# The down projection of a decoder layer, product by product over all pairs of k tiles, with operands formed earlier and read back from DRAM

## The chip, the core and the metric

The kernel runs on one core of one Trainium2 chip. The time is what the device takes for one execution, in microseconds (us), and the figure that counts is the median of several executions. The core's engines are told by their names in the profile: PE (matrix products; PEld its weight loads), DVE (vector), ACT (scalar), POOL (GpSimd), SP (which here only issues transfers). SBUF is the memory on the core, PSUM the eight banks that PE writes, DRAM the memory outside.

## The reference

One inference step of one hybrid decoder layer for 1024 prompt tokens and 32 sample tokens (1056 columns in all), all in float32. The part that matters here is the end of the layer, the gated MLP and the final norm:

```
up = rmsnorm(x, ln2) @ ffn_up                    # 1024 -> 2 * 2816
upc, ff_new = causal_dwconv(up, ff_prev, ffn_conv_w)
gate, val = jnp.split(upc, 2, axis=-1)
x = x + (jax.nn.silu(gate) * val) @ ffn_down     # 2816 -> 1024
y = rmsnorm(x, ln_f)
```

What comes before (three parallel mixers: attention, a short convolution, a gated delta net; their gates and the output projection) is computed by the same kernel and is left as it is.

## The kernel before

Everything is kept feature-major: 128 features on the partitions, 1056 tokens along a row. A float32 product is made of three products of float32r parts: every operand is split into hi and lo (`split`, L216: ACT casts hi, then DVE or POOL subtracts to get lo), and PE forms hi\*hi + hi\*lo + lo\*hi. One such matmul is 128x128 by 264 columns (a quarter of the tokens, HU; half of them, 528 columns, is HT).

Background work is written as generators, "lanes", that a loop advances by one step at each `bg.tick()` between matmuls, or without matmuls in `bg.until(cond)`. SBUF slots come from two arenas, `col` (24 slots) and `bg` (18). A lane that wants slots waits until there are enough. So the order in which the lanes were written out, and how many slots are free, fix the order of instructions on each engine; the engines take theirs strictly in that order. All loads and stores of the last stages go through SP's queue, except the weights, which ACT's queue issues.

The stages at the end:

- The up projection (from about 1228 us): 22 steps f, each with seven products in Winograd's form of Strassen's recursion (halves of features, of k tiles, and of tokens). While step f+1 runs, the lane `halves(f)` does the convolution, the SiLU and the product of step f, and writes the hidden features of k tile f to `hid_d[f]`.
- The down projection (`down_phase`, L2329) in the same form: pairs p of k tiles (2p, 2p+1), seven products i of sums of their quarters. Ten of eleven pairs are done so, in groups of 3, 4 and 3. Within a group, product i of all its pairs is summed in eight PSUM banks, and at the end of each group and product the eight banks are added to sums in SBUF (L2366 to L2368). The operands are made as the work goes on: `down_produce` (L2257) forms on DVE the sum of weights (L2286) and the sum of hidden features (L2291) that a product needs, then splits both (weights' lo on POOL, hidden features' lo on DVE). `together` (L2311, L2317) adds the partial sums to the residual `x1`.
- The last two k tiles (`last_group`, L2423, matmuls at L2437) without the recursion, by token groups, and behind each group the final norm of its token blocks (`final_block`, transposes at L2409).

Of the kernel before, what the change touches and what calls it, by code (L numbers as in the profile page):

```python
# [6 lines left out]
F32 = mybir.dt.float32  # L7
# [34 lines left out]
def shape_constants():  # L42
    """Identity, triangles and masks: they depend on the shapes alone."""
# [31 lines left out]
class Lanes:  # L75
    """Background work, traced in steps between the matrix products of the projections."""
# [45 lines left out]
class Arena:  # L122
    """SBUF slots of one size; a slot is free again after its tile's last use."""
# [27 lines left out]
XT_ACT = 1, 4, 7   # k tiles whose x^T the scalar engine copies  # L151
# [9 lines left out]
v b3 k q1 q2 q3 attn_in attn z0 z1 z2 z3  # L161
# [5 lines left out]
DITEM, DAHEAD = 4, 3  # L167
KEEP = 1
# [5 lines left out]
def trunk(tc, A, O, cst_d):  # L174
# [40 lines left out]
    def split(src, hi, lo, eng):  # L215
        """hi + lo == src exactly, each in the 12 significant bits that float32r carries."""  # L216
# [12 lines left out]
    # matrices of q = head * 8 + chunk: A's diagonal and off-diagonal blocks, (I + A)^-1 of the diagonal ones, U  # L229
# [23 lines left out]
    smallT = cp.tile([128, 40], F32, name="smallT")  # L253
# [48 lines left out]
    def look():  # L302
        """The next weights, from within a step."""
# [16 lines left out]
    def products(ps, wh, wl, xh, xl, nk, tg):  # L320
        """ps[:, :TG] = w.T @ x over nk k tiles: float32 products of exact hi + lo parts."""
# [18 lines left out]
    def group(tg):  # L340
        """columns of the group, its prompt columns, its samples"""
# [4 lines left out]
    def padded(t, K):  # L346
        """[128, 8, K - 1 + 4] view of the samples' rows behind the padded prompt."""
# [3 lines left out]
    def conv(src, K, w, out):  # L351
        """Causal depthwise conv along the padded columns; out column o reads o .. o + K - 1."""
# [8 lines left out]
    def conv_samples(t, K):  # L361
        """[128, 8, 4] view of the samples' columns of a conv output."""
# [3 lines left out]
    def state_in(src, rows, nct, dst, name):  # L366
        """(rows, nct * 128) -> dst[128, nct * rows], columns (ct, row), through the tensor engine."""
# [19 lines left out]
    def state_out(src, R, nct, pr, out_p, out_s, name):  # L387
        """src[128, nct * R], per ct pr prompt rows, then the samples' rows, to the two state outputs."""
# [24 lines left out]
    # =============== h = rmsnorm(x), feature-major, as hi + lo ===============  # L413
# [10 lines left out]
    ss, rs, fs = smallT[:, 4:13], smallT[:, 13:22], smallT[:, 22:40]  # L424
# [1715 lines left out]
    def halves(f, gc, uc):  # L2140
# [44 lines left out]
        if f >= NFT - 2:  # L2185
            ta.drop()
# [301 lines left out]
```

## Time and profile before

| what | value |
|---|---|
| median of 3 runs | 1954.34 us (1954.75, 1948.69, 1954.34) |
| span of the profiled execution | 1948.5 us |
| that span against the runs | 0.2 us below the lowest of them, 5.8 us below the median |
| PE busy in the span | 1820.2 us (93%) |
| DVE busy | 1360.4 us (70%) |
| POOL busy | 1017.4 us (52%) |
| ACT busy | 793.9 us (41%) |
| DRAM and SBUF traffic | 251.24 MB, 129 GB/s on average |

A row that begins with an interval gives the busy time of each engine in it and, in brackets, its number of instructions; PEclk is the mean granted clock of PE as a share of full speed. In a row of a group of instructions come the busy time, the mean duration of one in ns, and the idle time of the engine just before them with what ended it. An overlap of pipelined matmuls makes the duration of one longer than the distance between two.

### The profile page before, as it was taken

How to read it: one execution, taken by the hardware profiler on the slowest of the kernel's cores; microseconds unless marked ns; L12 is line 12 of the kernel's file. 1: busy time of each engine (PE TensorE's matmuls, PEld its weight loads, DVE VectorE, ACT ScalarE, POOL GpSimd, SP SyncE). 2: the span in 40 equal slices, each digit the busy share in tenths (PEclk: the TensorE clock that was granted, in tenths of full speed). 3: DMA queues.
4: the chain of work that ended last, by engine and by line, in shares of the span. 5: the costliest groups of instructions: out<-in, count | busy, mean ns of one | idle time of the engine just before them, and what ended most of it. 6: DMA issues, size and time to landing. Idle time of an engine off the chain costs nothing. (4 is left out here: it accounts for less than half of the span.)

```text
span 1948.5 us, 33487 instructions
## 1 busy us (share of the span) xinstructions
PE 1820.2 (93%) x12822; PEld 1760.5 (90%) x12822; DVE 1360.4 (70%) x2385; ACT 793.9 (41%) x1644; POOL 1017.4 (52%) x936
## 2 busy tenths in 40 slices
PE   6999899989999999989898999999999999989878
PEld 5888799989989998989787998999999999879877
DVE  5689845822447677766999757766666667986895
ACT  5654511011124444334544455545545444523312
POOL 1565666613213213363568547777777774544761
PEclk8999999988999999989999999999999999999979
DMA  6312876475745436432553342222322226512102
GB/s 218 108 60 84 286 230 192 107 192 163 228 126 152 135 101 202 166 109 96 202 179 111 121 144 88 87 79 67 99 67 83 82 67 238 190 36 100 45 12 106
DMA packets 265471, 251.24 MB, mean 129 GB/s; under 512 B 55698, under 2 KB 225150, under 8 KB 265294
## 3 DMA queue, kind: packets, MB, share of 16 engines
q1 hardware_dynamic: 209278, 208.20, 33.2%
q10 hardware_dynamic: 56032, 40.90, 7.0%
q8 instruction: 101, 1.65, 0.3%
q14 instruction: 60, 0.49, 0.1%
HBM read 176.23 MB, written 74.82 MB: 129 GB/s over the span
## 5 line engine op out<-in xcount | busy, mean ns | idle before, releaser
L326 PE MATMUL mm<-col,wh 128*128 128x352 f32 x2424 | 607.0, 329 | 17.5 <-DVE col L1203 13.7
L326 PEld LDWEIGHTS mm<-col,wh 128*128 128x128 f32 x2424 | 428.3, 191 | 26.1 <-issue 11.3
L326 PE MATMUL mm<-col,wl 128*128 128x352 f32 x1224 | 401.5, 328 | 0.0
L218 POOL TENSOR_TENSOR wl<-wr,wh 128x1024 fp32r<-128x1024 f32 x50 | 124.0, 2479 | 238.6 <-ACT wh L217 209.4
L326 PEld LDWEIGHTS mm<-col,wl 128*128 128x128 f32 x1224 | 232.9, 190 | 2.8 <-issue 0.5
L217 ACT CAST wh<-wr 128x1024 fp32r<-128x1024 f32 (+2 forms) x100 | 79.7, 803 | 178.4 <-PE mm L326 157.2
L218 POOL TENSOR_TENSOR wl<-col,wl 128x512 fp32r<-128x512 f32 (+1 forms) x78 | 101.8, 1305 | 96.2 <-ACT wl L217 89.3
L218 POOL TENSOR_TENSOR wh<-col,wh 128x512 fp32r<-128x512 f32 (+1 forms) x74 | 97.4, 1316 | 73.1 <-ACT wh L217 63.9
L1449 DVE TENSOR_TENSOR bgps<-bgps,col 128x264 f32<-128x264 f32 x136 | 59.2, 437 | 96.9 <-PE bgps L1421 91.7
L1421 PE MATMUL mm<-bg,wh 128*128 128x264 f32 x744 | 114.0, 289 | 7.4 <-DVE wh L218 2.5
L1421 PE MATMUL mm<-col,wh 128*128 128x264 f32 x648 | 105.1, 290 | 10.9 <-ACT col L1430 5.2
L1421 PE MATMUL mm<-bg,wl 128*128 128x264 f32 x720 | 109.3, 288 | 4.6 <-DVE wl L218 2.2
L1421 PEld LDWEIGHTS mm<-bg,wh 128*128 128x128 f32 x744 | 100.8, 192 | 9.5 <-DVE wh L218 2.9
L1421 PEld LDWEIGHTS mm<-bg,wl 128*128 128x128 f32 x720 | 96.9, 191 | 5.9 <-DVE wl L218 2.4
L1421 PEld LDWEIGHTS mm<-col,wh 128*128 128x128 f32 x648 | 90.4, 193 | 12.8 <-ACT col L1430 5.8
L1421 PE MATMUL mm<-col,wl 128*128 128x264 f32 x576 | 95.1, 292 | 6.8 <-POOL wl L218 3.3
L217 ACT CAST wh<-col 128x512 fp32r<-128x512 f32 (+1 forms) x86 | 48.1, 562 | 113.7 <-PE bgps L1421 59.0
L1421 PEld LDWEIGHTS mm<-col,wl 128*128 128x128 f32 x576 | 81.4, 194 | 8.0 <-POOL wl L218 3.5
L359 DVE SCALAR_TENSOR_TENSOR col<-col,vecT 128x1080 f32<-128x1080 f32 (+1 forms) x44 | 81.7, 1873 | 5.1 <-ACT col L357 3.3
L1421 PE MATMUL bgps<-col,wl 128*128 128x264 f32 x528 | 84.2, 288 | 1.0 <-POOL wl L218 1.0
L1203 DVE TENSOR_TENSOR col<-mm,bg 128x352 f32<-128x352 f32 x84 | 43.4, 517 | 56.6 <-PE mm L326 56.4
L217 ACT CAST wl<-col 128x512 fp32r<-128x512 f32 (+1 forms) x92 | 51.9, 566 | 75.1 <-PE mm L2355 32.2
(578 smaller groups left out, 4964.0 us busy)
## 6 DMA issues: line engine op xcount, KB each, us to landing
wr<-in_w_in SPq DMA_DIRECT2D x44, 512.0 KB
g_d<-col SPq DMA_DIRECT2D x24, 528.0 KB
wr<-in_ffn_up ACTq DMA_DIRECT2D x22, 512.0 KB
col<-in_ffn_up ACTq DMA_DIRECT2D x22, 512.0 KB
hid_d<-col SPq DMA_DIRECT2D x21, 512.0 KB
bg<-qkv_d SPq DMA_DIRECT2D x40, 256.0 KB
col<-g_d SPq DMA_DIRECT2D x18, 528.0 KB
col<-hid_d SPq DMA_DIRECT2D x13, 528.0 KB
```

The source lines that it names most:

```text
L217: nc.scalar.copy(hi, src)
L218: eng.tensor_tensor(lo, src, f32(hi), op=ALU.subtract)
L326: mm(ps[:, :TG], a[:, k, :], b[k][:, cc], start=n == 0, stop=n == last)
L359: nc.vector.scalar_tensor_tensor(out[:, :L], src[:, j:j + L], w(j), out[:, :L], op0=ALU.mult, op1=ALU.add)
L1203: nc.vector.tensor_tensor(dst[:, cc], ps[:, :TG], rr1[:, cc], op=ALU.mult)
L1421: mm(ps, w[:, x + k, :], b[y][:, c0:c0 + HU], start=not n and piece not in NESTED, stop=n == last, skip_group_check=piece in NESTED)
L1449: nc.vector.tensor_tensor(dst, ps, x, op=ALU.add)
```

## The change

The down projection is written anew. All eleven pairs take part in the recursion. One product is done for all eleven pairs before the next begins (order t1, b22, b11, t2, t3, t4, b21), summed over the pairs in eight PSUM banks. A chain of products goes on in the same banks: t1 then b22, and b11 then t2, t3, t4; where a product ends, the banks are added to the right quarter of the residual, while the sum in them goes on. So `together`, the sums in SBUF over groups and the last group without recursion are gone. The last product, b21, is done by token quarters, and the final norm follows behind.

The operands of a product and a pair are one item, and they are read from DRAM as they are needed: a quarter of weights (128x512) and of hidden features (128x528), or sums of such quarters. The sums of weights are formed by a new lane `weight_sums` on POOL, beside the attention and the gates; the sums of hidden features by `halves` on DVE, behind each odd step f of the up projection. `down_load` reads eight items ahead, `down_produce` splits four ahead. All of these transfers are on SP's queue. The `bg` arena has 21 slots instead of 18; the scratch memory for DMA descriptors is set to 1024.

```diff
-N_COL, N_BG = 24, 18
+N_COL, N_BG = 24, 21
-DITEM, DAHEAD = 4, 3
+DITEM, DAHEAD, DLOAD = 4, 4, 8
...
-v b3 k q1 q2 q3 attn_in attn z0 z1 z2 z3
+v b3 k q1 q2 q3 attn_in attn sums z0 z1 z2 z3
...
+    def weight_sums():
+        for p in range(NPAIR):
+            yield sb.room(3)
+            wa, wb, s = (sb.take([128, 1024]) for _ in range(3))
+            for i, w in enumerate((wa, wb)):
+                dma(w, A["ffn_down"][0][(2 * p + i) * 128:(2 * p + i + 1) * 128, :])
+            yield bg.arrived()
...
+            tt = nc.gpsimd.tensor_tensor
+            tt(s1, a21, a22, op=ALU.add)
+            tt(s2, s1, a11, op=ALU.subtract)
+            yield
+            tt(a21, a11, a21, op=ALU.subtract)
+            tt(a12, a12, s2, op=ALU.subtract)
+            yield bg.after(4.0)
+            for x, t in (("t1", s1), ("t2", s2), ("t3", a21), ("b22", a12)):
+                dma(sw_d[x][p], t)
...
     def halves(f, gc, uc):
...
-        dma(hid_d[f][:, 0:SEQ], gv[:, 0:SEQ])
-        dma(hid_d[f][:, SEQ:T], h.rearrange("p b t -> p (b t)"))
+        nc.scalar.copy(bt(gv[:, SEQ:T]), h)
...
+        if f % 2 == 0:
+            dma(hp_d["b11"][p], gv[:, :HT])
+            first_hid[p] = gv, va
+            return
...
+        for x, c in (("b21", 0), ("b22", HT)):
+            dma(hp_d[x][p], gb[:, c:c + HT])
...
+        sub(t1, b12, b11)
+        dma(hp_d["t1"][p], t1)
+        yield between
+        sub(t2, b22, t1)
+        dma(hp_d["t2"][p], t2)
+        yield between
+        sub(b12, b22, b12)
+        dma(hp_d["t3"][p], b12)
+        yield between
+        sub(b11, b21, t2)
+        dma(hp_d["t4"][p], b11)
...
-    GROUPS = (3, 4, 3)
...
+    def down_load(j):
+        while dn["loaded"] <= min(j, len(items) - 1):
+            n = dn["loaded"]
+            x, p = items[n]
+            bg.until(lambda: room2(1)() and (n >= NPAIR or done.get("hid", 0) > p))
+            t, ta = grab([128, SLOT])
+            w, b = t[:, 0:512], t[:, 512:512 + HT]
...
+            dma(w, src)
+            dma(b, hp_d[x][p])
...
+    def down_produce(j):
...
+            b, ba = grab([128, T], F32R)
+            split(bs, b[:, :HT], b[:, HT:T], nc.vector)
+            split(ws, w[:, :512], w[:, 512:], nc.gpsimd)
...
-    def together():
...
+    def down_mm(ps, w, b, mp, u, start, stop):
...
+        mm(ps, hi, bh, start=start, stop=False, skip_group_check=True)
+        mm(ps, hi, bl, start=False, stop=False, skip_group_check=True)
+        mm(ps, lo, bh, start=False, stop=stop, skip_group_check=True)
+
+    def down_out(x, ps, mp, u):
+        dm, c = DOUT[x]
+        o = x1[mp + dm][:, c + u * HU:c + (u + 1) * HU]
+        with tc.high_priority(offset=PRI_PAIR):
+            nc.vector.tensor_tensor(o, o, ps, op=ALU.add)
...
     def down_phase():
...
+        for j in range(end):
+            x, p = items[j]
+            down_load(j + DLOAD)
+            down_produce(j + DAHEAD)
...
+            for n, (mp, u) in enumerate(tiles):
...
+                down_mm(ps, w, b, mp, u, p == 0 and x in ("t1", "b11"), p + 1 == NPAIR)
+                if p + 1 == NPAIR:
+                    down_out(x, ps, mp, u)
+                bg.tick(us=0.33)
...
+        for u in range(2):
...
+            for i in range(3):
+                bg.add(final_block(5 + 3 * u + i, u * HU + 88 * i, 88))
...
-    def last_group():
...
-    nc = _bacc.Bacc("TRN2", target_bir_lowering=False, num_devices=1)
+    nc = _bacc.Bacc("TRN2", target_bir_lowering=False, num_devices=1, dynamic_dma_scratch_size=1024)
```

Where instructions stand now. First DVE in the middle of the down projection, before: L2291 is a sum of hidden features, L2286 a sum of weights, L218 the lo part of a split, L2368 the addition of a PSUM bank to a sum in SBUF.

```order
L2291 TENSOR_TENSOR bg<-col,bg 128x528
L2291 TENSOR_TENSOR col<-col 128x528
L218 TENSOR_TENSOR col<-bg,col 128x528
L2291 TENSOR_TENSOR col<-bg,col 128x528 x2
L2291 TENSOR_TENSOR bg<-col,bg 128x528
L2286 TENSOR_TENSOR col<-wr,bg 128x512
L2286 TENSOR_TENSOR col<-col 128x512
L2286 TENSOR_TENSOR wr<-wr 128x512
L218 TENSOR_TENSOR col<-col 128x528
L2286 TENSOR_TENSOR col<-col 128x512
L2368 TENSOR_TENSOR col<-col,bgps 128x264
L2368 TENSOR_TENSOR col<-col,mm 128x264
```

The same engine in the same stage now: L217 is the lo part of a split, L2347 the addition of a bank to the residual.

```order
L217 TENSOR_TENSOR col<-col 128x528
L2347 TENSOR_TENSOR col<-col,mm 128x264
L217 TENSOR_TENSOR col<-col 128x528 x10
L2347 TENSOR_TENSOR col<-col,bgps 128x264
L2347 TENSOR_TENSOR col<-col,mm 128x264
L2347 TENSOR_TENSOR col<-col,bgps 128x264 x2
L2347 TENSOR_TENSOR col<-col,mm 128x264
L2347 TENSOR_TENSOR col<-col,bgps 128x264 x2
L217 TENSOR_TENSOR col<-col 128x528
```

The sums have left this stage; between two products' additions stand some eleven splits, one for each pair.

The sums of hidden features stand on DVE in the up projection, behind an odd step f: L2180 and L2200 are the convolution and the gating product (L2155 and L2175 before), L2222 the new sums, L1448 and L2259 the additions and the scaling that empty PE's banks (L1449 and L2208 before).

```order
L2180 SCALAR_TENSOR_TENSOR bgps<-col,sfcw,bgps 128x356
L2200 TENSOR_TENSOR col<-col,bgps 128x356
L2222 TENSOR_TENSOR col<-col 128x528
L1448 TENSOR_TENSOR bgps<-bgps,col 128x264
L2222 TENSOR_TENSOR col<-col 128x528 x2
L2259 TENSOR_TENSOR bg<-bgps,col 128x264
L2222 TENSOR_TENSOR col<-col 128x528
L1448 TENSOR_TENSOR bgps<-mm,col 128x264
L2259 TENSOR_TENSOR bg<-bgps,col 128x264
```

Four sums have come in among the instructions that empty the banks.

Last, SP's queue where the up projection ends and the down projection begins: `ht1_d10` is the t1 sum of the hidden features of the last pair (written, then read for the eleventh item), `ht2_d10` to `ht4_d10` its other sums, `sb22_d` and `hb22_d` the operands of the product after it.

```order
L182 DMA ht1_d10_343<-col_18177 128x528
L182 DMA col_18219<-hb22_d0_355 128x528
L182 DMA ht2_d10_354<-col_18177 128x528
L182 DMA ht3_d10_376<-col_17743 128x528
L182 DMA col_18252<-sb22_d1_433 128x512
L182 DMA col_18252<-hb22_d1_356 128x528
L182 DMA ht4_d10_398<-col_17743 128x528
L182 DMA col_18285<-sb22_d2_434 128x512
L182 DMA col_18285<-hb22_d2_357 128x528
L182 DMA col_18318<-sb22_d3_435 128x512
L182 DMA col_18318<-hb22_d3_358 128x528
L182 DMA col_18186<-ht1_d10_343 128x528
```

Before, the last pair's features (`hid_d20`, `hid_d21`) were read near the end of the stage; now they are read within the first product, behind ten other transfers and three more writes.

## Rows read from the trace of the kernel before

**Rows 1.** The page's part 1: busy time, share of the span, instructions
```profile
PE 1820.2 (93%) x12822; PEld 1760.5 (90%) x12822; DVE 1360.4 (70%) x2385; ACT 793.9 (41%) x1644; POOL 1017.4 (52%) x936
```

**Rows 2.** Windows by stage: interval, its length, busy us (instructions) of each engine, clock, DMA
```profile
core 0: us, PE busy (x) PEld busy (x) DVE busy (x) ACT busy (x) POOL busy (x), PEclk, DMA share, GB/s
450.00:800.00 350.00, 350.00 (x2167) 320.00 (x2166) 199.15 (x363) 123.19 (x285) 90.10 (x66) 0.99 0.54 161
800.00:1228.00 428.00, 391.11 (x2752) 382.34 (x2751) 334.79 (x541) 201.76 (x421) 254.04 (x196) 0.96 0.39 130
1228.00:1620.00 392.00, 392.00 (x3237) 392.00 (x3237) 260.20 (x598) 192.20 (x440) 285.67 (x365) 1.00 0.25 80
1645.66:1906.90 261.24, 224.13 (x1681) 219.71 (x1682) 224.42 (x321) 95.09 (x182) 138.53 (x84) 0.92 0.25 87
1906.90:1936.80 29.90, 29.90 (x208) 29.43 (x207) 19.52 (x45) 9.90 (x33) 2.72 (x5) 1.00 0.27 98
1936.80:1948.50 11.70, 2.10 (x20) 1.74 (x18) 6.98 (x18) 3.01 (x11) 2.15 (x4) 0.70 0.49 193
```

**Rows 3.** Windows of one line's matmuls: L1421 (up projection), then L2353 (down)
```profile
1400.00:1600.00 200.00, 200.00 (x1653) 200.00 (x1652) 1.00 0.26 81
...
1645.66:1906.90 261.24, 154.64 (x560) 107.34 (x560) 0.92 0.25 87
```

**Rows 4.** PE's waits from 1640 us on: us in total, times, longest us
```profile
PE bgps L2353 <- DVE col L2368: 27.9, 8, 8.1
PE bgps L2354 <- DVE col L218: 4.6, 3, 3.5
```

**Rows 5.** Groups by form, 1645 to 1948.5: count, busy us, mean ns, idle before
```profile
L218 POOL TENSOR_TENSOR wh<-col,wh 128x512 fp32r<-128x512 f32 x25 | 38.3, 1532 | 23.9 <-ACT wh L217 21.7 <-issue 2.2
L218 DVE TENSOR_TENSOR col<-col 128x528 fp32r<-128x528 f32 x34 | 37.1, 1096 | 2.7 <-ACT col L217 2.6
...
L217 ACT CAST col<-col 128x528 fp32r<-128x528 f32 x34 | 21.1, 632 | 8.1 <-DVE col L2291 2.4 <-POOL bg L218 2.3 <-POOL wh L218 1.7
L2368 DVE TENSOR_TENSOR col<-col,bgps 128x264 f32<-128x264 f32 x50 | 20.2, 420 | 8.6 <-PE bgps L2355 8.5
...
L2286 DVE TENSOR_TENSOR col<-col 128x512 f32<-128x512 f32 x12 | 12.6, 1049 | 0.0
...
L2155 DVE SCALAR_TENSOR_TENSOR col<-bg,sfcw,col 128x358 f32<-128x358 f32 x4 | 4.3, 1082 | 0.1
```

**Rows 6.** DVE in order of time: start, us, line, tiles [idle before]
```profile
1605.25 4.20 DVE L2155 SCALAR_TENSOR_TENSOR bgps<-bg,sfcw,bgps 128x358 f32<-128x358 f32 x8
...
1614.06 0.44 DVE L1449 TENSOR_TENSOR bgps<-bgps,col 128x264 f32<-128x264 f32 x1 [1.04 <-PE bgps L1421]
...
1648.49 0.70 DVE L2291 TENSOR_TENSOR col<-col 128x528 f32<-128x528 f32 x1
...
1656.03 1.79 DVE L2291 TENSOR_TENSOR col<-col 128x528 f32<-128x528 f32 x1
...
1690.55 0.52 DVE L2175 TENSOR_TENSOR col<-col 128x356 f32<-128x356 f32 x1
```

**Rows 7.** SP's queue in order of time: start, us to issue, transfer, number
```profile
1645.70 3.87 SPq L183 DMA_DIRECT2D col<-x_d  x7
...
1692.13 0.58 SPq L183 DMA_DIRECT2D hid_d<-bg  x1
1694.71 0.32 SPq L183 DMA_DIRECT2D col<-hid_d  x1
```

**Rows 8.** The chain that ended last, its part of transposes: start, us, what
```profile
1916.71 1.09 PE bgps L2409 x10
```

**Rows 9.** Windows with transfers: columns as in the second group
```profile
400.00:440.00 40.00, 35.40 (x223) 34.85 (x222) 4.41 (x13) 5.44 (x9) 2.39 (x1) 0.83 0.81 195
1640.00:1660.00 20.00, 18.80 (x148) 17.96 (x147) 19.91 (x34) 10.26 (x24) 7.10 (x7) 1.00 0.88 336
1700.00:1720.00 20.00, 16.53 (x135) 16.22 (x133) 19.69 (x25) 8.10 (x15) 10.19 (x7) 0.99 0.38 139
```

More of the change, by code (lines that the diff above doesn't have):

```diff
@@ L1762, in trunk @@
     named["attn"] = lambda: step(bg_later)
+    named["sums"] = lambda: step(lambda: bg.add(weight_sums()))
     named["op1"] = lambda: step(lambda: bg.add(seq(attn_done(), load_operand(1, sb))))
@@ L2228, in up_phase @@
         ff["rr"][1].drop()
-    GROUPS = (3, 4, 3)
-    NPAIR = sum(GROUPS)
-    dn = {"w": {}, "h": {}, "items": {}, "s": {}, "loadedw": set(), "loadedh": set()}
-    subitems = [(g, i, p) for g, n in enumerate(GROUPS) for i in range(7) for p in range(sum(GROUPS[:g]), sum(GROUPS[:g]) + n)]
-    def down_load(g, keep=0):
-        if g >= len(GROUPS):
-            return
-        p0, n = sum(GROUPS[:g]), GROUPS[g]
-        queue = [(x, 2 * p + odd) for odd in range(2) for x, p in
-                 ([(x, p) for p in range(p0, p0 + n) for x in "wh"] if not odd else
-                  [(x, p) for x in "wh" for p in range(p0, p0 + n)])]
-        for x, k in queue:
-            if k in dn["loaded" + x]:
-                continue
-            wr = x == "w" and k % 2 == 0 and k < 2 * p0 + 4 and g % 2 == 0
-            if not wr and not room2(keep + 1)():
-                return
-            if wr:
-                t = cp.tile([128, 8, 128], F32, name="wr", tag="wr", bufs=2).rearrange("p a b -> p (a b)"), None
-            else:
-                t = grab([128, D if x == "w" else T])
-            dma(t[0], down[k * 128:(k + 1) * 128, :] if x == "w" else hid_d[k], nc.scalar if x == "w" else nc.sync)
-            dn[x][k] = t
-            dn["loaded" + x].add(k)
@@ new lines, in trunk @@
+    DPROD = ("t1", "b22", "b11", "t2", "t3", "t4", "b21")
+    DOUT = {"t1": (4, HT), "b22": (0, HT), "b11": (0, 0), "t2": (0, HT), "t3": (4, HT), "t4": (4, 0), "b21": (0, 0)}
+    items = [(x, p) for x in DPROD for p in range(NPAIR)]
+    dn = {"raw": {}, "items": {}, "loaded": 0, "made": 0}
+    last = {}
+    def down_load(j):
[5 more added lines that the diff above has]
+            w, b = t[:, 0:512], t[:, 512:512 + HT]
+            k, c = {"b11": (0, 0), "b21": (1, 0), "t4": (1, 512)}.get(x, (0, 0))
+            src = sw_d[x][p] if x in sw_d else down[(2 * p + k) * 128:(2 * p + k + 1) * 128, c:c + 512]
+            dma(w, src)
+            dma(b, hp_d[x][p])
+            dn["raw"][n] = w, b, ta
+            dn["loaded"] += 1
@@ new lines, in down_produce @@
+    def down_produce(j):
+        while dn["made"] <= min(j, len(items) - 1):
+            n = dn["made"]
+            down_load(n)
+            last_x = items[n][0] == DPROD[-1]
+            bg.until(room2(2 if last_x else 1))
+            ws, bs, ra = dn["raw"].pop(n)
+            if last_x:
+                w, wa = grab([128, 1024], F32R)
+            else:
+                tag = ("wh", "wl")[n % 2]
+                w, wa = cp.tile([128, 8, 128], F32R, name=tag, tag=tag, bufs=2).rearrange("p a b -> p (a b)"), None
+            b, ba = grab([128, T], F32R)
+            split(bs, b[:, :HT], b[:, HT:T], nc.vector)
+            split(ws, w[:, :512], w[:, 512:], nc.gpsimd)
+            ra.drop()
+            dn["items"][n] = w, b, [a for a in (wa, ba) if a]
+            dn["made"] += 1
@@ L2380, in trunk @@
-    last = {"h": [], "l": [], "gh": [], "gl": []}
-    def last_load():
-        for i in range(2 * NPAIR, NFT):
-            for src, names, n in ((down[i * 128:(i + 1) * 128, :], ("h", "l"), D), (hid_d[i], ("gh", "gl"), T)):
-                yield lambda: room2(3)() and done.get("hid", 0) > i
-                raw = grab([128, n])
-                dma(raw[0], src)
-                for k in names:
-                    last[k].append(grab([128, n], F32R)[0])
-                yield bg.arrived()
-                split(raw[0], last[names[0]][-1], last[names[1]][-1], nc.gpsimd)
-                raw[1].drop()
```

211 lines of the change are left out of this document (68 added, 143 removed).

## The prediction

> **What bounds the kernel now.** First the busy shares: PE is busy 93% of the span [rows 1], so a change gains only where PE is kept waiting or slow. Next the windows by stage show where that is [rows 2]. From 450 to 800 us and in the up projection (1228 to 1620) PE is busy all the time, with DVE at 199 of 350 and 260 of 392 us. In the down projection (1645.66 to 1906.90) it is busy 224 of 261 us at a mean granted clock of 0.92, and DVE 224. The last two k tiles and most final norms take 29.9 us at full clock, and 11.7 us pass after them.
>
> How fast PE could be is read from one line alone: 1653 matmuls of 264 columns in 200 us, 0.121 us each [rows 3]. The down projection has 560 records on each of three lines, 1680 in all: 203.3 us at that pace, against 261.2. So 57.9 us are lost there: 37.1 idle, the rest at the lower clock that goes with the gaps. The waits name the cause [rows 4]: 27.9 us for DVE to add a finished bank to SBUF (L2368), one of them 8.1 us. The addition itself takes 0.42 us [rows 5]; it stands in DVE's queue behind sums and splits of 1.05 and 1.10 us. DVE is the bound of this stage.
>
> **What goes.** In the stage itself, per DVE's list: 40 sums of hidden features and 40 of weights, `together`, two thirds of the bank additions (7 products times 8 banks is 56, where three groups had 168, 32 of them on ACT). Left are 77 splits x 1.10 = 84.7 and 56 x 0.42 = 23.5 us, 108 in all besides what remains of the up projection. ACT casts 2 x 0.63 an item, POOL has one lo part of 1.53. An item is 24 matmuls, 24 x 0.121 = 2.9 us, so each engine but PE has slack, and the clock should stay at 1.0 (2.4 GHz) as in the up projection.
>
> **What PE has to do.** 11 pairs x 7 products x 24 = 1848 matmuls x 0.121 = 223.6 us. The final norm goes over 11 blocks of 8 transposes, and 6 transposes belong to a state output: 94 x 0.109 [rows 8] = 10.2 us.
>
> **What is late next.** (a) The first item. SP's first read now stands behind the write of features of step 20; in the trace the transfers behind that write begin at 1645.70 [rows 7]. Landing takes about 2.0 us (the write issued until 1692.71 was waited for until 1694.71 [rows 7]), a cast 0.63, a split 1.10: 3.7 us. The half that is written needs only the first pieces of the step, so it can be sooner: 1 to 5, I take 3.
> (b) The features of step 21, due in the first product. DVE has seven splits, twelve convolution instructions, three gating products and the first sum ahead of the seventh item's lo part: 7 x 1.10 + 12 x 1.08 + 3 x 0.52 + 1.0 = 23 us from about 1649, so 1673 for an item due at 1666. With the undisturbed durations (0.70 a split or sum, 4.20/8 = 0.53 a convolution instruction [rows 6]) it is 14 us and nothing is late. The eleventh item is read behind ten transfers (x 0.55 = 5.5 us, from 3.87 for 7 [rows 7]) and lands about 1681 against 1678. If step 21 ended as late as before, at 1691.07 [rows 6], the item would come at 1691.1 + 5.5 + 2.0 + 0.6 = 1699, 21 us late. Bounds 0 and 21, taken 5, near the middle of the two reckonings from durations (0 and 7).
> (c) Six times a product ends and the banks go on: eight additions 3.4 us against a round of PE over eight banks of 2.9, with a split of 1.1 in between: 0 to 1.6 each, I take 0.5, 3 in all.
> (d) The last product's first pass takes 11 x 12 x 0.121 = 16 us, beside five blocks of the final norm. In the 29.9 us where six blocks and 24 additions ran, DVE did 19.5 us of work and PE had no gap [rows 2]; now seven splits come on top (four are made ahead), 7.7 us. 0 to 7.7, taken 3.
> (e) The tail after the last matmul, now 11.7 us [rows 2] with three blocks behind it: three blocks of 88 tokens, 11.7 to 16, taken 12.5.
>
> **What moves ahead.** The 44 sums of hidden features stand in DVE's queue of the up projection, among the additions that free PE's banks. DVE idles 132 of 392 us there [rows 2]; a run of 4.20 us and what follows it still leave DVE waiting 1.04 us for PE [rows 6]. Four sums of 0.70 to 1.79 us eat that and more, in 11 steps. With one product of 2.9 us of lead in banks PE may lose nothing; if each sum delayed PE in full it is 44 x 1.79 = 79 us. I take 0.4 a pair, 4 us, near the side of the row that shows PE without a gap. If the cover is gone, each us that a pair costs PE is 11 us.
> The 44 sums of weights on POOL, 44 x 1.53 = 67 us, fall mostly in 450 to 800 us, where POOL is busy 90 of 350 and PE does not wait. Their 22 loads and 44 writes go past the weight loads in SP's queue, which are two jobs ahead (two times 72 matmuls). The three slots more change the order of lanes from the first 100 us on. The trace shows no such case: bounds from -10 (a quarter of the 37 us that PE idles in 800 to 1228) to +37 (that idle time doubled), taken 0.
>
> **The transfers.** An item is 532 KB, so 41 MB in some 224 us, 185 GB/s, in 256 KB pieces, where the trace has moved 336 GB/s at a share of 0.88 and 195 at 0.81 in small pieces [rows 9]. At the first, loads cost PE nothing; at the second, the margin is 5%. I take nothing, by the first, since rows of 2 KB are nearer to it.
> The Trainium skill speaks against it (DMA: Bandwidth & Descriptors, section Bandwidth): single transfers should be 1 MB or more for three quarters of the peak. It also states a fixed part of about 2 us for each transfer that GpSimd issues (section Anatomy of one DMA); the 2.0 us of a write that SP issued [rows 7] agree. Whether the fixed parts lie beside each other decides; seven transfers of 528 KB were issued in 3.87 us, so here they do. By the rule without overlap the sum is that of the slow rival below.
>
> **Sum.** From 1645.66: 223.6 + 10.2 + 3 + 5 + 3 + 3 + 12.5, and 4 from the up projection, is 264.3: a span of 1910.0, 38.5 less than now. The profiled span is 0.2 us below the lowest run and 5.8 below the median of 1954.34. Shifted by that the median would be 1915.8, without it 1910; I predict 1913.
>
> **Rivals.**
> *The last pair holds the first product up.* (b) at its upper end: SP's queue is in order, so what waits there for a sum on DVE holds the next product's loads too. Speaks for it that step 21 ended 45 us after the up projection before; against it that DVE then made operands for ten items, which it doesn't now. 16 us more: 1929.
> *The sums move the bound into the up projection.* If half of the 44 sums of 1.0 us land on PE: 22 us instead of 4, 1931. For it: PE's banks are freed by the same DVE. Against: 132 us idle there.
> *The early stages eat the gain.* More slots and a lane more reorder the attention and the merge, where PE already idles 37 us. If that doubles: 1950, no change. For it: DVE at 335 of 428 us there. Against: the lane's work is on POOL, with 254 of 428.
> *Loads one after another.* If a transfer waits for the one before, an item costs 2 x (2.0 + 0.8 us for 264 KB at 336 GB/s) = 5.6 us, 77 x 5.6 = 431 us: some 2120, slower. From 77 x 3.7 = 285 us on (that is below 145 GB/s) the change is slower than before. For it: one queue, 154 loads, and a window at 139 GB/s [rows 9]. Against: that window had a DMA share of 0.38, so nothing was asked of it.
> That the change does not do what it says, so that DVE stays the bound in the stage, would need 2.9 us of DVE work an item; it has 1.4.
>
> **How the numbers follow.** Forecast 0.62, last pair 0.15, up projection 0.09, early stages 0.09, loads 0.05. Of the early-stages case 0.02 is still faster, 0.05 no change, 0.02 slower. What a measurement can tell from no change is about 0.3%, 6 us. So faster 0.62 + 0.15 + 0.09 + 0.02 = 0.88, same 0.05, slower 0.07. Range: all costs at their lower ends give 1645.66 + 223.6 + 10.2 + 1 + 11.7 = 1892, with some gain in the early stages 1886. Above, the last pair and the up projection together give 1945; 1946 leaves out the early-stage and load cases.
>
> **What would show it.** Right: PE at 0.121 us a matmul from some 30 us into the down projection, clock 1.0, DVE below 60% there, no wait of PE over 2 us behind the first product, its waits in that product for DVE's lo parts or a read of hidden features, and a PE busy share near 95%. Wrong: gaps of PE in the up projection before the L1448 additions; ACT waiting for loads in every item; the up projection's end later than 1645 us by more than the 4 us.

## The result, and the profile after

The changed kernel takes 1929.82 us (median of 4 runs, 1927.2 to 1930.73), the kernel before 1952.49 us beside it (1948.69 to 1954.75): a ratio of 0.9888, 95% interval 0.9867 to 0.9908. It is faster by 22.7 us. 1913 was forecast; the range of 1886 to 1946 holds the time, but 17 us are missing. The profiled execution has a span of 1928.6 us.

The page's part 1 after [rows 1]: PE is busy a little more of the span, DVE has 87 us less, POOL 28 us more. The traffic grew from 251.24 to 300.83 MB.

```profile
PE 1811.1 (94%) x12862; PEld 1749.3 (91%) x12862; DVE 1273.0 (66%) x2240; ACT 800.2 (41%) x1652; POOL 1045.3 (54%) x973
```

The windows by stage, shifted to the same stages of work [rows 2]:

```profile
450.00:800.00 350.00, 347.96 (x2159) 321.86 (x2158) 187.58 (x330) 111.11 (x247) 149.34 (x105) 0.98 0.71 214
800.00:1246.00 446.00, 408.46 (x2818) 393.14 (x2817) 361.66 (x578) 215.58 (x461) 266.93 (x212) 0.97 0.42 141
1246.00:1638.00 392.00, 392.00 (x3230) 391.60 (x3230) 298.60 (x632) 195.39 (x459) 293.48 (x359) 1.00 0.30 96
1664.30:1720.00 55.70, 47.37 (x365) 46.14 (x366) 37.54 (x48) 25.38 (x48) 22.37 (x17) 0.94 0.89 327
1720.00:1880.00 160.00, 160.00 (x1328) 160.00 (x1327) 60.69 (x102) 69.63 (x120) 72.78 (x57) 1.00 0.57 182
1880.00:1917.00 37.00, 34.06 (x251) 31.73 (x249) 15.44 (x35) 12.15 (x36) 8.33 (x10) 0.91 0.27 83
1917.00:1928.60 11.60, 0.64 (x4) 0.38 (x4) 4.95 (x12) 3.13 (x12) 1.61 (x3) 0.69 0.30 93
```

From 1720 to 1880 us the forecast of the stage is met: PE has no gap, a clock of 1.0, 1328 matmuls and transposes in 160 us (0.120 us each), and DVE is busy for 38%. The up projection pays nothing for the sums of hidden features: 3230 instructions in 392 us, where it had 3237, while DVE went from 260 to 299 us. The down projection takes 264.3 us (1664.3 to the end) instead of 302.8. But it begins at 1664.3 and not at 1645.66. The loss lies before it.

Where before it, is found by counting: add up PE's matmuls in windows of 20 us, and note when a given count is reached in each kernel. The difference to the kernel before is its lag. The changed kernel lags 16 us at 400 matmuls, 10 to 13 us up to 830 us, 18 us at 900 us, and, but for a dip to 13 near 980 us, 17 to 19 from there to the down projection. (A matmul that lies across the border of two windows counts in both. Two kernels with one order of instructions up to there differ by 2 to 4 us at single counts, so a smaller lag says nothing.) The first loss is a single wait of PE:

```profile
98.40 0.53 PE L622 MATMUL bgps<-bg,hot 128*48 128x352 f32 x1 [13.71 <-ACT bg L216]
```

The sums of squares (L622, L623 before) are a step of the stage's background work; before, the wait there was 3.15 us. ACT, in order of time, shows what stands ahead of the cast that PE wants (the second of the two in the row at 96.74, over at 98.35):

```profile
85.04 1.18 ACT L1786 ACTIVATE bg<-bg,vecT 128x1056 f32<-128x1056 f32 x1 [0.34 <-POOL bg L217]
...
91.23 1.18 ACT L1786 ACTIVATE bg<-bg,vecT 128x1056 f32<-128x1056 f32 x1 [1.60 <-POOL bg L1812]
...
94.79 1.18 ACT L1786 ACTIVATE bg<-bg,vecT 128x1056 f32<-128x1056 f32 x1 [2.38 <-POOL col L217]
96.74 1.61 ACT L216 CAST bg<-col 128x528 fp32r<-128x528 f32 x2 [0.78 <-DVE col L1803]
98.25 0.63 ACT L216 CAST col<-col 128x528 fp32r<-128x528 f32 x1
```

In the kernel before, the cast for the same sums of squares started at 84.93:

```profile
84.93 1.07 ACT L217 CAST col<-col 128x1056 fp32r<-128x1056 f32 x1
```

L1786 and L1803 belong to `h_build`, which forms operands for later products. Of its eight L1786, six stood ahead of that cast before, and now all eight do: `h_build` got the slots it asks for sooner, and ACT, in order, now waits for DVE and POOL in its name.

In the down projection PE's waits from 1660 us on have another head than before [rows 4]:

```profile
PE bgps L2339 <- ACT col L216: 8.9, 3, 6.1
PE bgps L2405 <- DVE col L2414: 3.3, 1, 3.3
```

### The profile page after: what moved, and what is told of

It is laid out like the page before. It is cut to its first block, busy times and chain, and to the rows that moved or that the text cites. A ratio compares the mean times of both kernels' runs of the same rounds, so it can differ in the third digit from the quotient of the medians.

```text
span 1928.6 us, 33928 instructions
## 1 busy us (share of the span) xinstructions
PE 1811.1 (94%) x12862; PEld 1749.3 (91%) x12862; DVE 1273.0 (66%) x2240; ACT 800.2 (41%) x1652; POOL 1045.3 (54%) x973
## 2 busy tenths in 40 slices
DMA packets 295571, 300.83 MB, mean 156 GB/s; under 512 B 56228, under 2 KB 225680, under 8 KB 295392
## 5 line engine op out<-in xcount | busy, mean ns | idle before, releaser
L325 PE MATMUL mm<-col,wh 128*128 128x352 f32 x2472 | 622.0, 330 | 8.4 <-DVE col L1202 3.1
L325 PE MATMUL mm<-col,wl 128*128 128x352 f32 x1248 | 409.8, 329 | 0.8 <-POOL wl L217 0.8
L325 PEld LDWEIGHTS mm<-col,wl 128*128 128x128 f32 x1248 | 238.3, 191 | 3.5 <-POOL wl L217 1.6
L217 POOL TENSOR_TENSOR wl<-wr,wh 128x1024 fp32r<-128x1024 f32 x50 | 124.8, 2496 | 187.7 <-ACT wh L216 177.7
L217 POOL TENSOR_TENSOR wl<-col,wl 128x512 fp32r<-128x512 f32 (+1 forms) x90 | 113.9, 1265 | 102.3 <-ACT wl L216 95.7
L217 POOL TENSOR_TENSOR wh<-col,wh 128x512 fp32r<-128x512 f32 (+1 forms) x82 | 102.3, 1247 | 85.0 <-ACT wh L216 74.3
L217 DVE TENSOR_TENSOR col<-col 128x528 fp32r<-128x528 f32 x72 | 59.2, 831 | 106.8 <-ACT col L216 95.5
L1420 PEld LDWEIGHTS mm<-bg,wh 128*128 128x128 f32 x786 | 105.1, 191 | 12.5 <-DVE bgps L1448 5.7
L216 ACT CAST col<-col 128x528 fp32r<-128x528 f32 (+1 forms) x113 | 69.6, 627 | 77.8 <-POOL wh L217 31.8
L1448 DVE TENSOR_TENSOR bgps<-bgps,col 128x264 f32<-128x264 f32 x136 | 58.5, 435 | 62.8 <-PE bgps L1420 61.5
L216 ACT CAST wl<-col 128x512 fp32r<-128x512 f32 (+1 forms) x104 | 59.6, 573 | 93.7 <-PE bgps L1420 29.2
L1420 PE MATMUL mm<-col,wl 128*128 128x264 f32 x534 | 87.3, 286 | 5.9 <-DVE bgps L1448 3.0
L2180 DVE SCALAR_TENSOR_TENSOR bgps<-col,sfcw,bgps 128x358 f32<-128x358 f32 (+1 forms) x168 | 89.4, 591 | 1.1 <-ACT bgps L2178 0.3
L1420 PE MATMUL bgps<-bg,wl 128*128 128x264 f32 x558 | 83.2, 289 | 0.5 <-ACT wl L216 0.5
```

The source lines that it names most:

```text
L216: nc.scalar.copy(hi, src)
L217: eng.tensor_tensor(lo, src, f32(hi), op=ALU.subtract)
L325: mm(ps[:, :TG], a[:, k, :], b[k][:, cc], start=n == 0, stop=n == last)
L1420: mm(ps, w[:, x + k, :], b[y][:, c0:c0 + HU], start=not n and piece not in NESTED, stop=n == last, skip_group_check=piece in NESTED)
L1448: nc.vector.tensor_tensor(dst, ps, x, op=ALU.add)
L2180: nc.vector.scalar_tensor_tensor(ps, cb[:, a + i:b + i], w(i), ps, op0=ALU.mult, op1=ALU.add)
```

## The experiments

Line numbers in a kernel with an edit differ by up to six. The table has for every run the median and the ratio to runs of before on the same chip, PE's lag at three counts (400, 5400 and 8200 matmuls, reached by the kernel before at 86, 896 and 1300 us), and the time from matmul 11000 (at 1635 us before) to the span's end.

| kernel | us | ratio (95%) | lag at 86 | at 896 | at 1300 | from 11000 on |
|---|---|---|---|---|---|---|
| before | 1952 | 1 | 0 | 0 | 0 | 313.8 |
| changed | 1929.82 | 0.9888 (0.9867–0.9908) | 15.6 | 18.1 | 17.7 | 276.1 |
| e1 before, 21 slots | 1943.19 | 0.9958 (0.9945–0.9971) | 14.8 | −1.8 | −1.3 | 305.3 |
| e2 changed, 18 slots at first | 1921.81 | 0.9845 (0.9819–0.9871) | 4.1 | 7.3 | 5.4 | 275.3 |
| e3 changed, b11 first | 1917.40 | 0.9824 (0.9797–0.9851) | 15.4 | 15.8 | 14.5 | 265.2 |
| e4 before, no operand sums | 1919.87 | 0.9839 (0.9810–0.9867) | 1.0 | −0.6 | 2.3 | 281.1 |
| e5 changed, no weight sums | 1918.26 | 0.9805 (0.9788–0.9823) | 16.1 | 4.2 | 6.1 | 275.4 |
| e6 = e2 + e3 | 1911.67 | 0.9778 (0.9763–0.9793) | −0.4 | 9.2 | 8.1 | 266.0 |
| e7 = e6, sums at 1130 us | 1920.51 | 0.9821 (0.9805–0.9837) | 1.5 | −2.4 | 13.7 | 266.0 |
| e8 = e6, sums in the up projection | 1906.58 | 0.9765 (0.9741–0.9788) | 0.9 | −2.0 | 1.3 | 265.1 |
| e9 = e6, no GpSimd sums | 1914.67 | 0.9815 (0.9787–0.9844) | 1.5 | 12.2 | 12.5 | 264.7 |
| e10 = e6, not in the account | 1918.98 | 0.9830 (0.9810–0.9851) | 1.0 | 13.8 | 15.7 | 264.6 |
| e11 = e6, turns and slots alone | 1901.81 | 0.9741 (0.9713–0.9770) | −0.1 | −2.5 | −0.4 | 265.9 |
| e12 = e10 without GpSimd sums | 1912.74 | 0.9797 (0.9766–0.9828) | −1.1 | 10.3 | 10.7 | 265.5 |

**e1, the slots alone.**

```diff
-N_COL, N_BG = 24, 18
+N_COL, N_BG = 24, 21
...
-    nc = _bacc.Bacc("TRN2", target_bir_lowering=False, num_devices=1)
+    nc = _bacc.Bacc("TRN2", target_bir_lowering=False, num_devices=1, dynamic_dma_scratch_size=1024)
```

> The kernel before with 21 SBUF slots instead of 18 for the background steps and nothing else of the change (the space comes from a smaller scratch of DMA descriptors, as the four raw weight tiles must stay). In the kernel changed, PE's count of instructions is 11 us behind from about 120 us on and 18 us behind from 900 us on. Theory (slots): steps that ask for slots start earlier and put ACT's work ahead of casts that PE waits for; then this kernel shows the same lag of 9 to 16 us between 120 and 850 us, and its time is 1958 to 1968 us. Rival (the list of steps or the new sums do it, not the slots): within 4 us of before, 1949 to 1957.

The early half of the theory holds: the same lag, and the same wait in PE's list:

```profile
PE bgps L623 <- ACT bg L217: 13.7, 1, 13.7
```

But neither theory foresaw the rest: the time, 1943.19, is below both ranges. The lag shrinks to 6 us by 830 us and is gone at 896: in between, up to 859 us, the kernel before has a wait of 9.1 us of its own, for a scaling (L1203) that empties a bank and stands on DVE behind the sums of `h_build`, and in e1 these two are mixed in another order and PE does not wait. The kernel is even 8 us faster than before; that gain lies in the down projection, shorter by 8.5 us, and why three slots help there was not tried. So the gap that the slots open does not last, because the kernel before is held up later and e1 is not; the question became what holds up the changed kernel there.

**e2, 18 slots until the sums of the weights begin.**

```diff
+    sb.n = 18
...
-    named["sums"] = lambda: step(lambda: bg.add(weight_sums()))
+    named["sums"] = lambda: step(lambda: (setattr(sb, "n", N_BG), bg.add(weight_sums())))
```

> The changed kernel with only 18 of its 21 SBUF slots in use until the step that forms the sums of the weights begins, and 21 from there. Theory (slots): the early lag of 11 us is gone, the second one (7 us, near 900 to 1110 us) stays: 1917 to 1921 us, 0.994 of the changed kernel. Rival (the lag comes from elsewhere, or what is won early is lost in a wait later): 1927 to 1932 us.

The theory holds, though 1921.81 is just above its range: PE's wait at the sums of squares is 3.2 us again, and the kernel is 8 us faster. (The smaller scratch for descriptors is still there, so it is the slots.) A lag of 5 to 7 us stays, from 860 us on.

**e3, another order of products.**

```diff
-    DPROD = ("t1", "b22", "b11", "t2", "t3", "t4", "b21")
+    DPROD = ("b11", "t2", "t3", "t4", "t1", "b22", "b21")
...
-            bg.until(lambda: room2(1)() and (n >= NPAIR or done.get("hid", 0) > p))
+            bg.until(lambda: room2(1)() and done.get("hid" if n >= NPAIR else "hid0", 0) > p)
```

> The changed kernel with another order of the seven products of the down projection: first the one whose features come from even steps alone, the two that need features of step 21 not first. Theory: PE lost about 11 us in the first product because the features of step 21 and the casts behind them on ACT came late (one wait of 6.07 us in the seventh item); with the order changed, that wait goes and the time is 1919 to 1923 us. Rival (the first product is slow because the operands of its items are formed while the last steps' own work fills DVE and ACT, whichever product is first): 1926 to 1931 us, with the gap elsewhere in the same 45 us.

b11 reads hidden features of even steps alone. (The edit also changes the order in which the tiles of the residual are read.) The wait is gone, and the stage is 10.9 us shorter (276.1 to 265.2). The time, 1917.40, is a little below the theory's range because this run also lags 3 us less before the stage, which is scatter. In the changed kernel that wait looked like this; first DVE and then ACT in order of time. DVE ends the last gating product of step 21 (L2200), ACT's copy of it (L2205) waits for that, and behind the copy stand casts of operands that had nothing to do with step 21:

```profile
1685.59 2.25 DVE L2180 SCALAR_TENSOR_TENSOR col<-col,sfcw 128x356 f32<-128x356 f32 x2 [0.66 <-ACT col L2178]
1687.88 0.53 DVE L2200 TENSOR_TENSOR col<-col 128x356 f32<-128x356 f32 x1
```

```profile
1688.44 0.22 ACT L2205 COPY col<-col 128x32 f32<-128x32 f32 x1 [2.37 <-DVE col L2200]
1688.57 0.63 ACT L216 CAST col<-col 128x528 fp32r<-128x528 f32 x1
```

```profile
1689.25 0.59 PE L2339 MATMUL bgps<-col,wh 128*128 128x264 f32 x1 [6.07 <-ACT col L216]
```

With b11 first, PE's list of waits between 1660 and 1720 us is this and no more:

```profile
PE bgps L2340 <- ACT col L216: 1.7, 1, 1.7
PE bgps L2341 <- DVE col L217: 0.8, 3, 0.3
```

**e4, the kernel before without operand sums.**

```diff
-        src = (a11, s, s, a21, s, a12, a22)[i]
-        if 0 < i < 5:
-            x, y = ((a21, a22), (s, a11), (a11, a21), (a12, s))[i - 1]
-            nc.vector.tensor_tensor(src, x, y, op=ALU.add if i == 1 else ALU.subtract)
+        src = (a11, a21, a21, a21, a12, a12, a22)[i]
...
-        src = (b11, t, t, b12, b22, b21, t)[i]
-        if i in (1, 2, 3, 6):
-            x, y = {1: (b12, b11), 2: (b22, t), 3: (b22, b12), 6: (b21, t)}[i]
-            nc.vector.tensor_tensor(src, x, y, op=ALU.subtract)
+        src = (b11, b12, b22, b12, b22, b21, b21)[i]
```

> The kernel before with the seven sums per pair on DVE (and the four on GpSimd that go with them) left out: each product takes a plain quarter in place of a sum, so the output is another; all splits, casts, products, bank additions and PE's work stay. Theory (DVE's sums and splits hold up the bank additions): the down projection shortens by most of the 58 us that PE loses there, to a time of 1900 to 1920 us; what is missing to 1895 belongs to the last k tiles. Rival (the bank additions themselves and the change of banks every product bound the stage, so the products' order and the eight chained banks are what the change gains by): 1940 to 1950 us.

The edit takes out eight sums a pair, four of weights and four of hidden features, all of them on DVE; the expectation miscounts them. 1919.87 is at the upper edge of the theory's range, 20 us below the rival's. The stage loses 32.7 us with nothing but DVE's sums gone; the whole change takes 37.7 out of it. PE's wait for the bank addition (here L2362), 27.9 us before [rows 4], is halved:

```profile
PE bgps L2347 <- DVE col L2362: 14.0, 3, 6.0
```

So the reading of the stage was right: the additions were late because of sums and splits ahead of them on DVE. The chained banks alone were not tried.

**e5, the changed kernel without weight sums.** The step does nothing.

```diff
-    named["sums"] = lambda: step(lambda: bg.add(weight_sums()))
+    named["sums"] = lambda: step(lambda: None)
...
-            src = sw_d[x][p] if x in sw_d else down[(2 * p + k) * 128:(2 * p + k + 1) * 128, c:c + 512]
+            src = down[(2 * p + k) * 128:(2 * p + k + 1) * 128, c:c + 512]
```

> The changed kernel with the step that forms sums of the weights left out (22 loads, 44 GpSimd sums, 44 writes); the four products that read them take a plain quarter of the weights, so the output is another. The 21 slots stay. The kernel before with 21 slots also fell 11 us behind early, but was level again at the up projection; the changed kernel was not. Theory (the sums keep the attention from catching up): the early lag of 10 to 15 us is there up to 300 us, and the count of PE at the start of the up projection is within 4 us of before; time 1910 to 1916 us. Rival (the sums cost nothing, the lag stays for another reason, such as the place of the steps in the list): 1926 to 1932 us.

1918.26 lies between the two ranges: 11.6 us of the lag go at 1300 us, 6 stay. So the sums cost most of what was not caught up. That the slots cost the other 6 us is not shown here, since e1, with the same slots, had caught up. Where the attention's last mask addition on DVE (L1615, L1616) starts tells when the attention ends: 851 us in the changed kernel, 811 in e5, 806 in e1. (It is 797 in the kernel before, which waits 9.1 us all the same; so the end of the attention does not decide alone, the order of `h_build` behind it does as well.)

**e6, both edits.** The diffs of e2 and e3 together.

> Both edits that made the changed kernel faster at once: 18 slots until the sums of the weights begin, and the product of even-step features first. If the two losses are apart in time and causes, the gains add: 8 + 12 us off 1929.8 is 1910, so 1906 to 1913. If the second only moved work that the first had made late, 1914 to 1920.

The gains add. What is left of the lag grows from 4 to 9 us between 830 and 896 us, at one wait of PE near 870 us:

```profile
PE mm L1421 <- DVE col L1203: 9.6, 1, 9.6
```

DVE is busy 38.59 of 40 us there, with `h_build` and the end of the attention's softmax side by side. The sums of the weights run from 550 to 840 us beside that attention.

**e7 and e8, the sums later.** e7 begins them at the output projection (`yield lambda: done.get("wo")` ahead of the loop); e8 spreads them over the up projection:

```diff
         for p in range(NPAIR):
-            yield sb.room(3)
+            yield lambda: sb.live + 3 <= sb.n and done.get("hid0", 0) > max(0, p - 2)
```

> The same, with the sums of the weights begun only at the output projection (about 1130 us), behind the attention and the merge. Theory (the sums are what delays the attention): the wait of PE near 850 to 880 us, 7.9 us long with the sums beside the attention, is shorter or gone, and the lag of 5 us at the up projection goes to 0 or below: 1902 to 1909 us. Rival: GpSimd's 67 us and the transfers then disturb the output or the up projection, where GpSimd also makes operands: the same time as the kernel with both edits or up to 15 us more, with PE below 331 matmuls in 40 us.

> Both edits (18 slots until the sums' place in the list, the product of even-step features first), and the sums of the weights moved into the up projection, one pair of k tiles for about every two of its steps. With the sums begun at 1130 us PE's count was level with before at that point (8 us ahead of where it is with the sums beside the attention), and then 14 us were lost between 1160 and 1280 us, where the 11 pairs were formed at once. Theory (the sums cost what they delay, and at this pace GpSimd, busy 29 to 30 of 40 us there, has room): the gain of about 8 us stays, 1901 to 1907 us, with PE at 331 matmuls in 40 us through the up projection. Rival (GpSimd's operands of the up projection come late whenever a sum stands before them): PE loses 0.5 to 1.5 us a pair of k tiles, and with it most of the gain: 1908 to 1918 us.

e7: the theory was right about the wait near 870 us, the rival about the time, 9 us more than e6's. The wait and with it the lag are gone (−2.4 against 9.2), and then some 15 us are lost between 1140 and 1300 us, where the pairs' loads and GpSimd's sums come all at once. Two windows of e7:

```profile
1160.00:1200.00 40.00, 35.68 (x229) 34.48 (x227) 26.87 (x31) 18.35 (x32) 32.71 (x23) 1.00 0.68 238
1200.00:1240.00 40.00, 33.40 (x229) 32.47 (x230) 23.60 (x40) 18.44 (x39) 36.63 (x40) 0.83 0.54 170
```

e8 keeps most of it: 1906.58 is in the theory's range, though not quite for its reason. The up projection isn't free; it loses some 3 us, with 2771 matmuls in 340 us (2805 in e6) where POOL goes from 254 to 296 us:

```profile
1280.00:1620.00 340.00, 336.55 (x2771) 335.83 (x2770) 261.77 (x545) 170.65 (x404) 295.64 (x348) 1.00 0.45 149
```

It is the fastest complete kernel here, 23 us below the changed one; its interval and e6's overlap.

**e9 to e12, what in the sums delays the attention.** Four things come with the step: GpSimd's 67 us, its turns (the places that the loop gives it among the other steps) and slots, its transfers, and the transfers in the planner's account. That account is code (`Lanes`): every transfer adds its bytes at 360 KB per us, and while it is over 8 us, a `bg.tick()` takes no step but those of `h_build`. e9 drops the four GpSimd sums; e10 keeps them and hides the transfers from the account; e11 keeps turns and slots alone, the slots only in the planner's count, since it takes no buffer; e12 is e10 without the sums. The edit of e10:

```diff
+            was = bg.busy
             for i, w in enumerate((wa, wb)):
                 dma(w, A["ffn_down"][0][(2 * p + i) * 128:(2 * p + i + 1) * 128, :])
-            yield bg.arrived()
+            ready, bg.busy = bg.arrived(), was
+            yield ready
...
+            was = bg.busy
             for x, t in (("t1", s1), ("t2", s2), ("t3", a21), ("b22", a12)):
                 dma(sw_d[x][p], t)
+            bg.busy = was
```

> Both edits, with the 44 sums on GpSimd left out of the step that forms the sums of the weights; its loads, slots, waits and 44 writes stay in place (plain quarters are written, so the output is another). It parts GpSimd's 67 us from the step's slots, turns and transfers, all beside the attention. If GpSimd's time is what delays the attention: the wait of PE of 9.6 us near 870 us goes and the lag at the up projection with it, 1902 to 1907 us. If it is the slots, the turns among the background steps or the transfers: the wait stays at 7 to 10 us, 1909 to 1914 us.

> Both edits, and one number of the planner: the loads and writes of the weight sums no longer enter its account of the DMA queue (at 360 KB per us some 5.8 us per pair of k tiles), by which it lets background steps rest while the account is over 8 us and puts off every step that waits for loads; the sums' own step waits by the same estimate as before. Nothing is done in other places or by other engines. Theory (the account puts off the attention's steps): the attention's last mask addition on DVE comes before 815 us instead of 842, the wait of PE of 9.6 us near 870 us goes, the lag at the up projection is 0 to 3 us instead of 8: 1901 to 1907 us. Rival (real transfers in the queue, or turns and slots, delay the attention): the wait stays, 1909 to 1914 us; or, the account being right, steps now wait on engines for loads that have not landed, with new waits between 550 and 850 us: 1912 to 1925 us.

> Both edits, with the weight sums' step left as a shell: it takes its turns and holds its three slots as long by the planner's clock, but has no loads, GpSimd sums or writes (four products read plain quarters, so the output is another). If turns and slots delay the attention, PE's wait of 9.6 us near 870 us stays, 1909 to 1914 us. If the transfers do it, in the queue or in the planner's account of it: the wait goes, 1900 to 1907 us. Beside the run in which only the account is changed it shows what the real transfers and GpSimd's 67 us cost: nothing if both times are within 3 us.

> Both edits, the account of the planner without the transfers of the weight sums, and the 44 sums on GpSimd left out (the writes store plain quarters, so the output is another). Left are turns, slots and the real 22 loads and 44 writes. With account and transfers but no sums the time was 1914.7 us, with transfers and sums but no account 1919.0, with neither transfers nor sums nor account 1901.8. If the real transfers cost nothing once the account does not count them, and the 1919.0 came from sums that stood on GpSimd ahead of other operands at 835 to 846 us: 1900 to 1906 us, without a wait of PE over 3 us between 840 and 920 us. If the real transfers themselves delay loads that the engines wait for: 1910 to 1920 us.

e9: it is not GpSimd. The wait near 870 us stays, 8.7 us long, and the time, 1914.67, is just above the second range. e11: nor is it turns, or slots as the planner counts them. The wait goes, the lag is −0.4, and the time 1901.81 is the lowest of all. e10: my theory of the account falls. The attention's last addition does move, from 842 to 819 us, but the time gets worse by 7 us. In e10 POOL, in order of time, has the last sums between the operands of `h_build` (L1790, L218) that DVE, ACT and at last PE wait for:

```profile
834.97 1.30 POOL L2072 TENSOR_TENSOR bg<-bg 128x512 f32<-128x512 f32 x1 [3.54 <-DMA bg<-in_ffn_down]
836.21 2.99 POOL L1790 TENSOR_TENSOR bg<-col 128x1056 f32<-128x1056 f32 x1
839.16 1.29 POOL L2073 TENSOR_TENSOR bg<-bg 128x512 f32<-128x512 f32 x1
840.40 1.77 POOL L2075 TENSOR_TENSOR bg<-bg 128x512 f32<-128x512 f32 x1
```

e12 takes these away too. It needs 1912.74, 6.2 us less than e10, but still as much as e6 and 10.9 us more than e11. What it adds to e11 is the 22 loads and 44 writes, and that they hold three real buffers until the writes have landed. Two windows of e11 and then of e12 show them:

```profile
800.00:820.00 20.00, 20.00 (x122) 18.62 (x121) 14.74 (x28) 11.62 (x28) 4.66 (x2) 1.00 0.30 94
...
840.00:880.00 40.00, 37.31 (x248) 36.17 (x247) 32.64 (x35) 16.49 (x29) 29.16 (x17) 1.00 0.42 141
```

```profile
800.00:820.00 20.00, 20.00 (x114) 17.47 (x112) 12.46 (x20) 7.32 (x17) 3.69 (x2) 1.00 0.83 285
...
840.00:880.00 40.00, 33.03 (x204) 31.96 (x203) 38.48 (x35) 14.55 (x22) 29.00 (x15) 0.92 0.37 126
```

In e12 the DMA share is 0.83 where e11 has 0.30, ACT and DVE do less there, the attention ends at 821 us instead of 805, `h_build` starts its last part (L1790) at 838 instead of 821, and PE pays after 860 us. Whether the attention's own loads are slowed by the traffic itself, stand behind the sums' transfers in SP's queue, or wait for buffers that these still hold stays open. SP waited 18.4 us in nine waits for loads of the sums between 550 and 840 us (none in e11), 3.4 of them from 780 us on. That speaks for the queue, but SP waits for much else in both runs. ACT waited once for a write of a sum, 2.4 us, up to 840.90.

## Why the prediction was right, and where it was not

**The bound.** "DVE is the bound of this stage" held (e4), and so did what PE has to do: at 0.121 us a matmul the forecast of the stage from its start to the end was 260.3 us (1910.0 less 4 and 1645.66), measured 264.3 and, ahead of it, the 1.5 us of (a). Of the signs for right one failed: PE's waits in the first product were for ACT's casts (8.9 us) and hardly for DVE's lo parts (0.9). And one for wrong came: the stage began 18.6 us later than at 1645.66, where 4 were allowed.

**The terms of the stage.** (a) The first item cost 1.5 us of waiting, 3 forecast. (b) The first product was mis-sized: 365 instructions in 55.7 us are 11.5 us more than at 0.121, against 5 forecast, within the bounds of 0 and 21. The seventh item came 6.1 us late; the reckoning with the profile's mean durations had 7 for it, and 5 was taken for the whole product. But it came by another road than DVE's queue: its cast, ready long before, stood on ACT behind a copy that waited for step 21 (e3). Step 21 itself did not end as late as the rival of the last pair needed: its gating product was done 24 us into the stage (1688.4 less 1664.3), before it was 45 (1691.07 less 1645.66). The last pair's own item, the eleventh, was 1.3 us late. Other gaps made 1 us, and for the other 3 PE was slower than 0.121, above all behind the wait, at a mean clock of 0.74 from 1689.25 to 1696. (c) Product ends cost nothing visible, 3 forecast. (d) The last pass cost about 7 us, near its upper bound of 7.7, 3 forecast: the state output's transposes wait for DVE and ACT one by one, and the clock falls after it. PE in order of time, two of these rows, and then PE alone in the windows around (busy time, clock, DMA):

```profile
1884.61 0.33 PE L396 MATMUL bgps<-ident,col 128*128 128x128 f32 x1 [0.55 <-DVE col L2414]
...
1888.46 0.69 PE L396 MATMUL bgps<-ident,col 128*128 128x128 f32 x2 [0.60 <-ACT bg L397]
```

```profile
1884.00:1889.00 5.00, 2.78 (x14) 0.83 0.43 153
1889.13:1894.10 4.97, 4.97 (x23) 0.50 0.50 149
1894.20:1917.00 22.80, 22.66 (x191) 1.00 0.22 66
```

(e) The tail took 11.6, 12.5 forecast. The up projection's term was 4 and measured 0: DVE's 132 us of idle time did cover 44 sums. Transfers cost PE nothing in the stage, as taken. From 1720 to 1880 us they moved 182 GB/s, about the 185 reckoned. From 1690 to 1702 us, where the pieces of 256 and 264 KB were alone, they moved 353 GB/s at a share of 1.00, against 389 from 1660 to 1680, where two fifths of the bytes came in pieces of 528 KB. The Trainium skill's rule that a transfer should have 1 MB for three quarters of the peak (DMA: Bandwidth & Descriptors, section Bandwidth) does not hold for these pieces, several of them in flight: the trace disagrees, and the slow rival of 2120 us fell with it.

**The step that failed** is the one on what moves ahead: "bounds from -10 … to +37, taken 0". It measured +17.7 us, inside its bounds, and makes up the whole miss of the span: 1910.0 − 1.5 + 6.5 − 3 + 4 − 1 − 4 + 17.7 = 1928.7, where 1928.6 was measured. Two causes are shown. The slots: 8 us (changed to e2), 6 us (e3 to e6). The sums of the weights: 11.5 us (changed to e5), 10 us (e6 to e11). By the ratios in the table, which allow for the chip, the slots are 8 and 9 us and the sums 16 and 7, so which is the larger is not shown. I had weighed the sums by POOL, "busy 90 of 350", and found room. POOL did have room (e9); the transfers had less, from a DMA share of 0.54 in 450 to 800 us [rows 2] to 0.71, and the attention, which runs there on loads of its own, was not asked. PE had no wait of more than 1.2 us there, before or after; the price came due near 870 us (e6). The rival "the early stages eat the gain" named the place; it was taken at twice the size and with a chance of 0.09. That the range held the time is partly luck: its upper end was made up from the last pair and the up projection, and left this rival out.

The rival that ended nearest, 1929 for the last pair, is right by its number alone: that mechanism cost 6 us more than forecast, not 16.

## What to carry to other kernels

Work that is "moved to where the engine is idle" must be weighed on every resource it takes along there, its transfers and buffer slots above all, and against the work that runs beside it even where PE never waits: a delay there is paid at the next place where two chains meet. Count the bottleneck's instructions over time in both traces; the lag tells at once in which stage a gain was lost, and one edit for each suspect then tells why. An order of products that starts with operands that are ready longest cost nothing and gave 11 us.

## What the runs showed of the hardware beyond that

After PE's wait of 13.71 us the clock was at the lower level for 7 us, then full; first the window before the wait, and then the two behind it (PE alone):

```profile
60.00:84.00 24.00, 22.46 (x141) 1.00 0.28 90
98.40:105.40 7.00, 5.73 (x19) 0.50 0.03 8
105.40:130.00 24.60, 24.60 (x159) 1.00 0.11 45
```

So a long wait cost some 3 us more than itself (5.73 us of work at half the pace); this is part of the lag of 15.6 us.

The same split got faster on both engines [rows 5]: 1096 to 833 ns on DVE, 1532 to 1304 ns on POOL, in these groups from 1664 to 1928.6 us:

```profile
L217 DVE TENSOR_TENSOR col<-col 128x528 fp32r<-128x528 f32 x71 | 58.5, 833 | 106.8 <-ACT col L216 95.5 <-DMA col<-ht_d 8.7 <-DMA col<-hb_d 1.9
...
L217 POOL TENSOR_TENSOR wh<-col,wh 128x512 fp32r<-128x512 f32 x33 | 43.0, 1304 | 59.9 <-ACT wh L216 52.2 <-issue 5.5 <-DMA col<-st_d 2.2
```

That DVE had less to do does not explain it: in e4 DVE is busy 69% of the stage (86% before), and its splits still take 1054 and 1090 ns in their two large groups. It goes with POOL's work at the same time. In the kernel before, in e4 and in the changed one, DVE's splits of 128x528 took 0.70 us on average where POOL was busy for less than a tenth of their time, and 1.39 to 1.41 us where it was for more than six tenths (by the traces' spans, which are rough on POOL). The kernel before has 25 of the first kind and 36 of the second in the stage, e4 20 and 26, the changed kernel 57 and 11.
